# Sample attention: bias added on VectorE, fewer PE visits; prompt attention: v products of two steps together, in one PSUM bank

## The chip, the cores and the metric

The kernel runs on one core of a Trainium2 chip. The metric is the device time of one execution in microseconds. Three runs of the kernel before gave 2920.92, 2932.04 and 2932.24 us; their median, 2932.04 us, is the time before.

## What is computed

One layer of a hybrid decoder runs for two groups of tokens that share all weights: a prompt of 2048 tokens, and 8 samples of 8 new tokens each, which attend to 8192 cached tokens in a paged cache. Everything is float32; the projections are computed as three float32r products (high and low parts).

```python
h = rmsnorm(x, norm_g) * (1 + scale) + shift
z = h @ w_in                                  # one wide input projection, 8200 columns
pu, pg, q, k, v, fl, ag, ch, cb, cc, cg, mg = split_cols(z)
# forgetting attention, 8 heads of 64: for the prompt causal, for the samples over cache + new tokens
s = q @ k * scale + lq - lk                   # lk: cumulated log-forget values per cached row and head
p = softmax(where(k_pos <= q_pos, s, -inf)); o = p @ v
# pooling branch A, attention branch B, short convolution branch C
merged = sig(ga) * (ya @ w_br_a) + sig(gb) * (yb @ w_br_b) + sig(gc) * (yc @ w_br_c)
out = rmsnorm(x + gate * (merged @ w_o), final_g)
```

## The kernel before, in words

**First stage: projection and sample attention.** `project` streams the 2048 + 64 tokens through `w_in`, in two halves of the tokens: for each output tile of 128 columns and each of 8 input tiles three matmuls (L350 to L352, high by high, low by high, high by low). SP loads each weight tile (`raw`), ScalarE and VectorE split it. Behind this stream a generator, `decode`, computes the samples' attention over the cache. `pump` advances it in proportion to the projected columns; a scheduler with a simulated timeline then fixes each engine's order, by readiness and program order.

There are 64 decode steps, 8 per sample. A step takes 8 pages (1024 cached rows, 8 heads): two gathers of k (`kg`, issued by POOL), four VectorE transposes to `kt`, a bias (`nbt`), scores in PSUM bank dS, softmax, four TensorE transposes of the probabilities, `pT`, and then two halves (i = 0, 1) of products with four gathered v tiles each (`v`, POOL; `v_bufs` = 4 buffers) into bank dO. The bias of a row is written to DRAM as a high and a low part (`s_nbh`, `s_nbl`), loaded as 64 rows (`nbt`), and two matmuls with a selection matrix (L964) put it under the scores, which accumulate on it (L969). L964 is a 64 by 128 tile of the array; L969 and the v products (L995) are 128 by 32 tiles, four of which run side by side; the projection uses 128 by 128. The code has four yields per step: after the scores, after the softmax and the transposes, after each half of the products.

**Second stage: prompt attention with the A and C branches as filler.** `attention` runs 8 heads of 20 steps; TensorE's order here is written out by hand. A step handles two streams, each one 128-row tile of keys against a 512-column block Q of queries (stream 0: blocks 0 and 3, stream 1: blocks 1 and 2). At step i the code issues, in this order: the scores of step i + 1 (L1245, L1246, two PSUM banks `st`), three matmuls of the next head's maxima (L1170, three banks `mx`), twelve matmuls of a branch as filler (L1371 to L1373), and the v products of step i (L1263; stream 0 into bank oA, partitions 0 to 63, stream 1 into bank oB, partitions 64 to 127; each call is two machine matmuls). ScalarE exponentiates scores into `pt`; POOL and VectorE add `pt` into row sums `acc`. When a block is done, ScalarE copies it to `oT` (two buffers) and SP writes it to `s_o`. After the first step of the next head, `sums` reduces the `acc` tiles with ones (L1278) into an `mx` bank, ScalarE copies that to `ls`, which uses the same two buffers as `oT` (L1281). A head's q and k operands are four loads of 64 by 2048 (`head_loads`, L1150), into one of two whole sets.

**Third stage.** Branch B and the output projection; the change touches only where its first chunk starts.

The PSUM banks in the second stage are st 2, ac 1, oA 1, oB 1, mx 3: all eight.

Of the kernel before, what the change touches and what calls it, by code (L numbers as in the profile page):

```python
# [18 lines left out]
P = 128  # L19
# [20 lines left out]
class Mixer:  # L40
# [5 lines left out]
    def pools(self):  # L46
# [15 lines left out]
        self.s_nbh = dt("s_nbh", [NB * NPG, NH, P])  # L62
        self.s_nbl = dt("s_nbl", [NB * NPG, NH, P])
# [3 lines left out]
    def setup(self):  # L67
# [12 lines left out]
        self.ks = self.dp.tile([P, 4, NS], F32, name="ks")  # L80
        self.vs = self.dp.tile([NS, BW], F32, name="vs")
# [772 lines left out]
    def decode_consts(self):  # L854
        nc, dp = self.nc, self.dp

        sel = self.stage("sel")[0:64, 0:256].rearrange("p (a b) -> p a b", b=P)
        self.sel = dp.tile([64, 2, P], F32R, name="sel")
        for part in range(2):
            q = slice(32 * part, 32 * part + 32)  # L860
            nc.gpsimd.iota(sel[q], pattern=[[4, 2], [1, 4], [8, 4], [0, 8]], base=0, channel_multiplier=-1,
                           allow_small_or_imprecise_dtypes=True)
        nc.vector.tensor_scalar(out=self.sel, in0=sel, scalar1=0.0, scalar2=None, op0=ALU.is_equal)

# [3 lines left out]
        for g in range(4):  # L868
# [12 lines left out]
        nc.gpsimd.affine_select(out=self.tri, in_=self.tri, pattern=[[-1, P]], compare_op=ALU.is_gt, fill=0.0,  # L881
                                base=0, channel_multiplier=1)
        nc.vector.memset(self.tri[64:128, 0:64], 0.0)

    def decode_bias(self):
# [3 lines left out]
        nc.sync.dma_start(idxl, I["page_table"].rearrange("(n b) g -> (b g) n", n=4).bitcast(U32))  # L889
# [3 lines left out]
        for n in range(4):  # L893
# [18 lines left out]
            hi, lo = self.stage(f"nbh{n}", F32R)[:, 0:1024], self.stage(f"nbl{n}", F32R)[:, 0:1024]  # L912
            nc.scalar.copy(hi, nb)
            V.tensor_tensor(out=lo, in0=nb, in1=hi.bitcast(F32), op=ALU.subtract)
            for d, x in ((self.s_nbh, hi), (self.s_nbl, lo)):
                nc.sync.dma_start(d[n * P : (n + 1) * P].rearrange("n h t -> n (h t)"), x.bitcast(F32))

    def decode(self):

# [5 lines left out]
        NC = 8  # L925

# [9 lines left out]
        vs = values(0)  # L936
        qbd = dp.tile([P, 16, 32], F32, name="qbd")
        nc.gpsimd.memset(qbd, 0.0)
        for b in range(NB):
# [6 lines left out]
            stat = dp.tile([P, 2, 2, NC], F32, tag="stat", bufs=2, name=f"stat{b}")  # L946
            ob = dp.tile([P, 2, HD, NC], F32, tag="ob", bufs=1, name=f"ob{b}")
            for c in range(NC):
                nbt = dp.tile([64, 2, P], F32R, tag="nbt", bufs=2, name=f"nbt{b}_{c}")
                for part, d in ((0, self.s_nbh), (1, self.s_nbl)):  # L950
                    src = d[b * NPG + 8 * c : b * NPG + 8 * c + 8].rearrange("(t g) h x -> (g h) t x", g=4)
                    nc.sync.dma_start(nbt[32 * part : 32 * part + 32].bitcast(F32), src)
                kt = dp.tile([P, 2, 2048], F32, tag="kt", bufs=1, name=f"kt{b}_{c}")
                for i in range(2):
                    kg = dp.tile([P, 2048], F32, tag="kg", bufs=2, name=f"kg{b}_{c}_{i}")
                    t = b * 16 + c * 2 + i
                    ind(kg, ck, self.idxk[:, t : t + 1])
                    for x in range(2):
                        V.transpose(out=kt[:, i, x * D : (x + 1) * D], in_=kg[:, x * D : (x + 1) * D])  # L959
                ktv = kt.rearrange("p i (j x r) -> p i j x r", j=4, r=32)  # L960
                S = self.psum("dS")
                Sv = S.rearrange("p (a i x) -> p a i x", a=2, x=P)
                for hh in range(2):
                    nc.tensor.matmul(Sv[:, hh], self.sel[:, hh], nbt, start=(hh == 0), stop=False)  # L964
                for hh in range(2):
                    for dh in range(2):
                        for h4 in range(4):
                            x = (4 * hh + h4) * 2 + dh
                            nc.tensor.matmul(Sv[32 * h4 : 32 * h4 + 32, hh], qbd[:, x], ktv[:, :, :, x],  # L969
                                             start=False, stop=(hh == 1 and dh == 1))  # L970
                yield
                S3 = S.rearrange("p (a x) -> p a x", a=2)
                m, l = stat[:, 0, :, c], stat[:, 1, :, c]
                V.tensor_reduce(out=m, in_=S3, axis=AX.X, op=ALU.max)
                nm = dp.tile([P, 2], F32, tag="nm", bufs=2, name=f"nm{b}_{c}")
                V.tensor_scalar(out=nm, in0=m, scalar1=-1.0, scalar2=None, op0=ALU.mult)
                pr = dp.tile([P, 2, 256], F32, tag="pr", bufs=1, name=f"pr{b}_{c}")
                for hh in range(2):
                    nc.scalar.activation(out=pr[:, hh], in_=S3[:, hh], func=AF.Exp, bias=nm[:, hh : hh + 1],
                                         accum_out=l[:, hh : hh + 1])  # L980
                pt = self.psum("dT")
                for hh in range(2):
                    for i in range(2):
                        x = hh * 2 + i
                        nc.tensor.transpose(out=pt[:, x * P : (x + 1) * P], in_=pr[:, hh, i * P : (i + 1) * P],
                                            identity=self.ident)
                pT = dp.tile([P, 4, 4, 32], F32, tag="pT", bufs=1, name=f"pT{b}_{c}")
                nc.scalar.copy(pT.rearrange("p x g (h q) -> p x h g q", q=NQ),
                               pt.rearrange("p (x h g q) -> p x h g q", x=4, h=4, g=4))
                yield  # L990
                O = self.psum("dO")
                for i in range(2):

                    def product(hh, g):
                        return nc.tensor.matmul(O[32 * g : 32 * g + 32, hh * 256 : hh * 256 + 256],  # L995
                                                pT[:, 2 * hh + i, g], vs[g][:, hh * 256 : hh * 256 + 256],
                                                start=(i == 0 and hh == 0), stop=(i == 1 and hh == 1))


                    with self.tc.issue_after(product(0, 3).ins):  # L1000
                        for x in (0, 1, 2, 4, 5, 6, 7):
                            product(x // 4, x % 4)
                    if (b * NC + c) * 2 + i + 1 < NB * NC * 2:
                        vs = values((b * NC + c) * 2 + i + 1)
                    if i == 0:
                        yield
# [217 lines left out]
    def attention(self, filler):  # L1224
# [68 lines left out]
        for x, (h, i) in enumerate(steps):  # L1293
            if h + 1 < NH:
# [4 lines left out]
                if i == 4:  # L1299
                    self.head_loads(h + 1)  # L1300
# [283 lines left out]
```

## Time and profile before

| | us |
|---|---|
| median of three runs | 2932.04 |
| profiled execution, its own time | 2928.24 |
| its span (first to last instruction) | 2926.5 |
| first stage, 0 to 1966 | 1966.0, TensorE busy 1926.2 |
| second stage, 1966 to 2617.6 | 651.6, TensorE busy 604.2 |
| third stage, 2617.6 to the end | 308.9, TensorE busy 287.6 |

TensorE's mean granted clock is 0.981 of 2.4 GHz. "Busy" counts a matmul from its start to its modelled end, and matmuls overlap, so the cost of one is read from the distance to the next start: 0.23 us for 512 columns at the full clock, though the row says 0.39 us. A gap between starts that is longer than that is either a wait (in brackets at the row's end) or a cost of TensorE itself. The column PEclk of a stretch is the granted clock as a share of full speed.

### The profile page before, as it was taken

The page shows a single profiled execution, that of the slowest core. Times are in us where ns is not written, and L with a number is a line of the kernel's source. Part 1 is how long each engine was busy: PE and PEld are TensorE (multiplying, and loading weights), DVE is VectorE, ACT ScalarE, POOL GpSimd, SP SyncE. Part 2 cuts the span into 40 slices and gives each one's busy share as a digit, 9 for nine tenths or more (in the row PEclk, how much of TensorE's full clock was granted, in tenths as well). Part 3 has the DMA queues.
Part 4 walks back from the last instruction along what each step waited for, and adds up shares of the span by engine and source line. Part 5 has one row for each costly group of instructions (what it writes and reads, how often), then busy time and mean ns, then how long its engine had stood idle before and what let it go on. Part 6 is the DMA issues. An engine that isn't in the chain of part 4 may idle for free.

```text
span 2926.5 us, 45656 instructions
## 1 busy us (share of the span) xinstructions
PE 2818.0 (96%) x17611; PEld 2162.3 (74%) x17611; DVE 1524.8 (52%) x2732; ACT 771.0 (26%) x1546; POOL 1060.9 (36%) x1210
## 2 busy tenths in 40 slices
PE   7999999999999999999999999999999999989998
PEld 4778888788878887777777777775666566758886
DVE  5465654564343345466655533226655556645554
ACT  4322221222222332222112122213333333332221
POOL 1112344453444332344444432003433343424332
PEclk9999999999999999999999999999999899989999
DMA  6776667778777867977776775624455545247542
GB/s 224 249 222 209 206 222 239 231 241 270 247 256 255 272 192 246 299 233 234 241 237 226 257 230 154 161 83 134 115 142 137 146 123 134 85 125 221 172 142 82
DMA packets 397309, 577.55 MB, mean 197 GB/s; under 512 B 45639, under 2 KB 303351, under 8 KB 377611
## 3 DMA queue, kind: packets, MB, share of 16 engines
q1 hardware_dynamic: 337123, 304.05, 36.0%
q0 software_dynamic: 59968, 270.57, 27.1%
q8 instruction: 139, 2.28, 0.3%
q14 instruction: 79, 0.65, 0.1%
HBM read 478.82 MB, written 95.60 MB: 196 GB/s over the span
## 4 chain that ended last, share of the span: by engine, by line
PE 79%; DMA 11%; DVE 3%; issue 3%; POOL 2%; ACT 1%; SPq 1%; DVEq 0%; POOLq 0%; ACTq 0%
PE ps_a L350 15%; PE ps_a L351 15%; PE ps_a L352 15%; PE ps_dO L995 4%; PE ps_dS L969 4%; PE ps_oA L1263 4%; DMA v<-in_cache_v,idxv 3%; PE ps_st L1245 3%; PE ps_mx L1170 2%; PE ps_ac L1373 2%; PE ps_ac L1372 2%; PE ps_ac L1371 2%; PE ps_st L1246 2%; DMA s_o<-oT 2%; PE ps_u L1475 1%
## 5 line engine op out<-in xcount | busy, mean ns | idle before, releaser
L350 PE MATMUL ps_a<-h,whi 128*128 128x512 f32 (+2 forms) x2560 | 921.6, 360 | 3.2 <-ACT whi L326 1.5
L351 PE MATMUL ps_a<-h,wlo 128*128 128x512 f32 (+2 forms) x2560 | 911.4, 356 | 0.9 <-DVE wlo L327 0.9
L352 PE MATMUL ps_a<-h,whi 128*128 128x512 f32 (+2 forms) x2560 | 909.7, 356 | 0.2 <-POOL h L306 0.2
L923 POOL DMA_INDIRECT v<-in_cache_v,idxv x512 | 513.9, 1004 | 735.3 <-PE ps_dO L995 593.4
L350 PEld LDWEIGHTS ps_a<-h,whi 128*128 128x128 f32 x2560 | 483.2, 189 | 99.3 <-issue 34.2
L351 PEld LDWEIGHTS ps_a<-h,wlo 128*128 128x128 f32 x2560 | 483.6, 189 | 70.0 <-issue 11.5
L352 PEld LDWEIGHTS ps_a<-h,whi 128*128 128x128 f32 x2560 | 482.9, 189 | 70.9 <-issue 10.9
L327 DVE TENSOR_TENSOR wlo<-raw,whi 128x1024 fp32r<-128x1024 f32 x128 | 160.4, 1253 | 273.7 <-ACT whi L326 273.2
L959 DVE STREAM_TRANSPOSE kt<-kg 128x1024 f32<-128x1024 f32 x256 | 296.3, 1211 | 8.3 <-DMA kg<-in_cache_k,idxk 8.1
L1173 DVE TENSOR_REDUCE mx<-ps_mx 128x1 f32<-128x512 f32 (+3 forms) x288 | 159.0, 594 | 135.4 <-PE ps_mx L1170 134.4
L1268 POOL TENSOR_TENSOR acc<-acc,pt 128x512 f32<-128x512 f32 (+2 forms) x134 | 157.9, 1178 | 148.4 <-ACT pt L1251 128.5
L1251 ACT ACTIVATE pt<-ps_st 128x512 f32<-128x512 f32 (+3 forms) x288 | 141.0, 525 | 251.8 <-PE ps_st L1246 246.1
L923 POOL DMA_INDIRECT kg<-in_cache_k,idxk x128 | 130.2, 1017 | 200.8 <-DVE kt L959 112.7
L326 ACT CAST whi<-raw 128x1024 fp32r<-128x1024 f32 x128 | 133.8, 1046 | 163.6 <-PE ps_a L352 95.2
L669 ACT ACTIVATE mg<-ps_a 128x512 f32<-128x512 f32 (+2 forms) x120 | 62.7, 522 | 401.6 <-PE ps_a L352 394.1
L1245 PEld LDWEIGHTS ps_st<-qq,kk 128*128 128x128 f32 x320 | 61.7, 193 | 134.4 <-issue 109.6
L1371 PE MATMUL ps_ac<-gh,wh 128*128 128x264 f32 x512 | 150.6, 294 | 8.8 <-ACT wh L1326 5.3
L995 PE MATMUL ps_dO<-v,pT 128*32 128x256 f32 x2048 | 146.0, 385 | 9.8 <-DMA v<-in_cache_v,idxv 9.6
L1268 DVE TENSOR_TENSOR acc<-acc,pt 128x512 f32<-128x512 f32 (+2 forms) x154 | 104.8, 683 | 90.8 <-PE ps_oB L1263 48.8
L1373 PE MATMUL ps_ac<-gl,wh 128*128 128x264 f32 x512 | 149.5, 292 | 0.5 <-DVE gl L1327 0.5
L1372 PE MATMUL ps_ac<-gh,wl 128*128 128x264 f32 x512 | 149.5, 292 | 0.1
L969 PE MATMUL ps_dS<-kt,qbd 128*32 128x256 f32 x2048 | 147.8, 386 | 0.0
(357 smaller groups left out, 4137.8 us busy)
## 6 DMA issues: line engine op xcount, KB each, us to landing
raw<-in_w_in SPq DMA_DIRECT2D x128, 512.0 KB
s_mg<-mg SPq DMA_DIRECT2D x72, 256.0 KB
t<-s_mg SPq DMA_DIRECT2D x64, 264.0 KB
x<-in_x_prompt SPq DMA_DIRECT2D x32, 512.0 KB
s_m<-t SPq DMA_DIRECT2D x64, 132.0 KB
wc<-in_w_cond SPq DMA_DIRECT2D x16, 512.0 KB
v<-in_cache_v,idxv POOLq DMA_INDIRECT x512, 4.7
m<-s_m SPq DMA_DIRECT2D x64, 128.0 KB
```

What stands on the lines that cost most here:

```text
L327: nc.vector.tensor_tensor(out=lo, in0=raw, in1=hi.bitcast(F32), op=ALU.subtract)
L350: nc.tensor.matmul(acc, whi[:, k], hh, start=(k == 0), stop=False)
L351: nc.tensor.matmul(acc, wlo[:, k], hh, start=False, stop=False)
L352: nc.tensor.matmul(acc, whi[:, k], hl, start=False, stop=(k == KT - 1))
L923: ind = lambda out, src, idx: nc.gpsimd.indirect_dma_start(out=out, out_offset=None, in_=src, in_offset=bass.IndirectOffsetOnAxis(ap=idx, ...
L959: V.transpose(out=kt[:, i, x * D : (x + 1) * D], in_=kg[:, x * D : (x + 1) * D])
L969: nc.tensor.matmul(Sv[32 * h4 : 32 * h4 + 32, hh], qbd[:, x], ktv[:, :, :, x], start=False, stop=(hh == 1 and dh == 1))
L995: return nc.tensor.matmul(O[32 * g : 32 * g + 32, hh * 256 : hh * 256 + 256], pT[:, 2 * hh + i, g], vs[g][:, hh * 256 : hh * 256 + 256], s ...
L1268: e.tensor_tensor(out=acc[h, Q][:, lo:512], in0=acc[h, Q][:, lo:512], in1=pt[:, lo:512], op=ALU.add)
L1371: nc.tensor.matmul(y, wh[:, k, cols], hi[:, k], start=(k == 0), stop=False)
L1372: nc.tensor.matmul(y, wl[:, k, cols], hi[:, k], start=False, stop=False)
L1373: nc.tensor.matmul(y, wh[:, k, cols], lo[:, k], start=False, stop=(k == 3))
```

## The change

VectorE adds the bias: it is stored once, in float32 (`s_nb`), and loaded as a 128 by 512 tile by four DMAs, each of which reads 4 rows and repeats each 8 times (`nbt`, one buffer now). One `tensor_tensor_reduce` per half adds it to the scores in PSUM and takes the maximum; before, one `tensor_reduce` took the maximum of both. The selection matrix and its matmuls are gone. To make the score rows fit, the page order inside a step changes (`tri`, `idxl`, eight small loads).

A decode step has two yields: the first half of the previous step's products and this step's scores, then the second half of the products and this step's transposes. `issue_after` puts the later piece behind the earlier one on TensorE. `v_bufs` grows from 4 to 7. `ks`, `vs` and `n_o` lose their own buffers.

In the prompt's attention the v products of two steps are issued together, at odd i, into one bank `o` with the streams on its two partition halves; `sums` has a bank of its own (`l`) and comes at i = 1, before the products. q and k come in 512-column chunks from rings of five buffers; `pt` has 9 buffers instead of 5. In the A and C filler the B weights are loaded after the second set of A and C weights, not before, and branch B's first chunk waits six filler turns instead of four.

```diff
-            hi, lo = self.stage(f"nbh{n}", F32R)[:, 0:1024], self.stage(f"nbl{n}", F32R)[:, 0:1024]
-            nc.scalar.copy(hi, nb)
-            V.tensor_tensor(out=lo, in0=nb, in1=hi.bitcast(F32), op=ALU.subtract)
-            for d, x in ((self.s_nbh, hi), (self.s_nbl, lo)):
-                nc.sync.dma_start(d[n * P : (n + 1) * P].rearrange("n h t -> n (h t)"), x.bitcast(F32))
+            dst = self.s_nb[16 * n : 16 * n + 16].rearrange("c g h (a i x) -> i a (c g) h x", a=2, i=2)
+            for i in range(2):
+                for a in range(2):
+                    src = nb[64 * i : 64 * i + 64, 512 * a : 512 * a + 512]
+                    nc.sync.dma_start(dst[i, a], src.rearrange("p (h x) -> p h x", h=4))
...
+        def scores(k):
+            b, c = divmod(k, NC)
+            if c == 0:
+                queries(b)
+            nbt = dp.tile([P, 2, 256], F32, tag="nbt", bufs=1, name=f"nbt{k}")
+            for h4 in range(4):
+                nc.sync.dma_start(nbt[32 * h4 : 32 * h4 + 32].rearrange("p a x -> p (a x)"),
+                                  self.s_nb[k, :, h4].unsqueeze(1).broadcast_to([4, NQ, 4 * P]))
...
-                for hh in range(2):
-                    nc.tensor.matmul(Sv[:, hh], self.sel[:, hh], nbt, start=(hh == 0), stop=False)
...
-                V.tensor_reduce(out=m, in_=S3, axis=AX.X, op=ALU.max)
+            for hh in range(2):
+                V.tensor_tensor_reduce(out=S3[:, hh], in0=S3[:, hh], in1=nbt[:, hh], scale=1.0, scalar=-3 * BIG,
+                                       op0=ALU.add, op1=ALU.max, accum_out=m[:, hh : hh + 1])
...
+            with self.tc.issue_after(product(0, 3).ins):
+                for x in (0, 1, 2, 4, 5, 6, 7):
+                    last = product(x // 4, x % 4)
+            with self.tc.issue_after(last.ins):
+                then()
...
+        n = NB * NC
+        vs, pT = values(0), None
+        for k in range(n + 1):
+            run = lambda: None
+            if k < n:
+                S, nbt, run = scores(k)
+            if k:
+                O = self.psum("dO")
+                vs = products(k - 1, 0, pT, O, vs, run)
+            else:
+                run()
             yield
+            nxt = []
+            if k < n:
+                pr = softmax(k, S, nbt)
+                run = lambda: nxt.append(transposes(k, pr))
+            else:
+                run = lambda: nxt.append(None)
+            if k:
+                vs = products(k - 1, 1, pT, O, vs, run)
+                evict(k - 1, O)
+            else:
+                run()
+            pT = nxt[0]
+            yield
...
-    def head_loads(self, h):
-        nc = self.nc
-        r = slice(h * HD, (h + 1) * HD)
-        qq, kk = self.qq[h % 2], self.kk[h % 2]
-        for dst, src in ((qq[0:64], self.s_ql), (kk[0:64], self.s_kh), (qq[64:128], self.s_qh), (kk[64:128], self.s_kl)):
-            nc.sync.dma_start(dst.bitcast(F32), src[r])
+    def head_chunk(self, h, x, is_q):
+        r, c = slice(h * HD, (h + 1) * HD), slice(x * 512, x * 512 + 512)
+        ring, use, top, low = ((self.qq, self.qc, self.s_ql, self.s_qh) if is_q else
+                               (self.kk, self.kc, self.s_kh, self.s_kl))
+        t = use[h, x] = ring[len(use) % 5]
+        for dst, src in ((t[0:64], top), (t[64:128], low)):
+            self.nc.sync.dma_start(dst.bitcast(F32), src[r, c])
...
+        qload = {4: 0, 6: 1, 10: 3}
+        kload = {5: 0, 14: 1, 18: 2}
...
+                nc.tensor.matmul(O[64 * s : 64 * s + 64, lo:512], v[:, kt], pt[:, lo:512],
...
-            L = self.psum("mx")
+            L = self.psum("l")
...
+            if h and i == 1:
+                self.head_chunk(h, 2, True)
+                self.head_chunk(h, 3, False)
...
-            values(h, cur)
-            if i == 0 and h:
+            if i == 1 and h:
                 sums(h - 1, (0, 1, 2, 3))
-            if h == NH - 1 and i == 8:
+            if h == NH - 1 and i == 9:
                 sums(h, (0, 1))
                 self.early = True
+            if i % 2:
+                values(h, prev)
+                values(h, cur)
+            prev = cur
...
-    m.st_bufs, m.sc_bufs, m.v_bufs, m.pt_bufs, m.raw_bufs = 4, 8, 4, 5, 1
+    m.st_bufs, m.sc_bufs, m.v_bufs, m.pt_bufs, m.raw_bufs = 4, 8, 7, 9, 1
-    m.banks(two, "ps2", st=2, ac=1, oA=1, oB=1)
+    m.banks(two, "ps2", st=2, ac=1, o=1, l=1)
-            yield from m.branch_b(c, 0 if c else 4)
+            yield from m.branch_b(c, 0 if c else 6)
```

TensorE, first stage, decode step 11 (`kt` are its k tiles, `v` and `pT` those of the step before), before:

```order
L352 MATMUL ps_a<-h_665,whi_4645 128x256
L964 MATMUL ps_dS<-nbt_3_4877,sel 128x256 x2
L969 MATMUL ps_dS<-kt_3_4880,qbd 32x256 x13
L995 MATMUL ps_dO<-v_3_4627,pT_2_4745 32x256
L995 MATMUL ps_dO<-v_0_4621,pT_2_4745 32x256
L995 MATMUL ps_dO<-v_1_4623,pT_2_4745 32x256
L995 MATMUL ps_dO<-v_2_4625,pT_2_4745 32x256
L995 MATMUL ps_dO<-v_0_4621,pT_2_4745 32x256
L995 MATMUL ps_dO<-v_1_4623,pT_2_4745 32x256
L995 MATMUL ps_dO<-v_2_4625,pT_2_4745 32x256
L995 MATMUL ps_dO<-v_3_4627,pT_2_4745 32x256
L969 MATMUL ps_dS<-kt_3_4880,qbd 32x256 x3
```

and now:

```order
L353 MATMUL ps_a<-h_489,whi_4665 128x256
L1011 MATMUL ps_dO<-v_3_4725,pT_4717 32x256
L1011 MATMUL ps_dO<-v_0_4719,pT_4717 32x256
L1011 MATMUL ps_dO<-v_1_4721,pT_4717 32x256
L1011 MATMUL ps_dO<-v_2_4723,pT_4717 32x256
L1011 MATMUL ps_dO<-v_0_4719,pT_4717 32x256
L1011 MATMUL ps_dO<-v_1_4721,pT_4717 32x256
L1011 MATMUL ps_dO<-v_2_4723,pT_4717 32x256
L1011 MATMUL ps_dO<-v_3_4725,pT_4717 32x256
L977 MATMUL ps_dS<-kt_4824,qbd 32x256 x16
L354 MATMUL ps_a<-h_489,wlo_4666 128x256
```

The two L964 matmuls are gone, and the scores stand whole behind the first half of the products. In the whole program, visits of TensorE to the decode's scores and products (with L964, between rows of other work) go from 176 to 152.

TensorE, second stage, the start of head 1 (`acc` of head 0 are summed there), before:

```order
L1263 MATMUL ps_oA<-acc_0_18216,vh_16452 64x512
L1263 MATMUL ps_oB<-acc_1_18222,vh_16452 64x512
L1278 MATMUL ps_mx<-acc_0_17549,onesc 32x512
L1278 MATMUL ps_mx<-acc_1_17555,onesc 32x512
L1278 MATMUL ps_mx<-acc_2_17730,onesc 32x512
L1278 MATMUL ps_mx<-acc_3_17618,onesc 32x512
L1245 MATMUL ps_st<-qq_17544,kk_17545 128x256
L1246 MATMUL ps_st<-q_1_16431,k_1_16433 128x256
L1245 MATMUL ps_st<-qq_17544,kk_17545 128x512
L1246 MATMUL ps_st<-q_1_16431,k_1_16433 128x512
L1263 MATMUL ps_oA<-pt_0_1_18257,vh_16452 64x384
L1263 MATMUL ps_oB<-pt_1_1_18263,vh_16452 64x512
```

and now:

```order
L1303 MATMUL ps_st<-qq_17625,kk_17626 128x256
L1305 MATMUL ps_st<-q_1_16494,k_1_16496 128x256
L1303 MATMUL ps_st<-qq_16497,kk_17626 128x512
L1305 MATMUL ps_st<-q_1_16494,k_1_16496 128x512
L1335 MATMUL ps_l<-acc_0_17631,onesc 32x512
L1335 MATMUL ps_l<-acc_1_17637,onesc 32x512
L1335 MATMUL ps_l<-acc_2_17807,onesc 32x512
L1335 MATMUL ps_l<-acc_3_17694,onesc 32x512
L1320 MATMUL ps_o<-acc_0_18298,vh_16533 64x512
L1320 MATMUL ps_o<-acc_1_18304,vh_16533 64x512
L1320 MATMUL ps_o<-pt_0_1_18343,vh_16533 64x384
L1320 MATMUL ps_o<-pt_1_1_18349,vh_16533 64x512
```

The sums come after another group of scores, write bank l, and four v products follow them. Over the stage the visits to v products and sums go from 159 to 80; behind this place now stand four scores, three maxima and twelve filler matmuls before the next scores. At nine places two groups of scores stand without other matmuls between them (three groups at the start); before there was one.

SP's queue around the copies of finished blocks (`s_o`) at the end of head 0, before:

```order
L1150 DMA qq_17544<-s_ql 64x2048
L1139 DMA k_1_16433<-s_kh 64x2048
L1141 DMA k_1_16433<-s_nlkh 1x2048
L1141 DMA k_1_16433<-s_nlkl 1x2048
L1142 DMA q_1_16431<-s_qh 64x2048
L1378 DMA s_m<-t_1_18950 128x264
L1150 DMA kk_17545<-s_kh 64x2048
L1150 DMA qq_17544<-s_qh 64x2048
L1150 DMA kk_17545<-s_kl 64x2048
L1273 DMA s_o<-oT_3_19032 64x512
L1273 DMA s_o<-oT_2_19036 64x512
```

and now:

```order
L1202 DMA qq_16498<-s_ql 64x512
L1190 DMA k_1_16496<-s_kh 64x2048
L1192 DMA k_1_16496<-s_nlkh 1x2048
L1192 DMA k_1_16496<-s_nlkl 1x2048
L1193 DMA q_1_16494<-s_qh 64x2048
L1444 DMA s_m<-t_1_19038 128x264
L1202 DMA qq_16498<-s_qh 64x512
L1202 DMA kk_16502<-s_kh 64x512
L1202 DMA kk_16502<-s_kl 64x512
L1330 DMA s_o<-oT_3_19126 64x512
L1330 DMA s_o<-oT_2_19130 64x512
```

Four loads of 64 by 2048 for q and k (qq, kk) stood ahead of `s_o`; now two q loads and two k loads of 64 by 512 stand there. The loads of the maxima (k_1, q_1) stay.

## Rows read from the trace of the kernel before

**Rows 1.** Stretch us; busy PE, PEld, DVE, ACT, POOL; clock; DMA share; GB/s.

```profile
200.00:1800.00 1600.00, 1588.84 (x11122) 1244.87 (x11121) 818.71 (x1133) 374.57 (x806) 667.96 (x662) 1.00 0.73 238
...
1966.00:2617.60 651.60, 604.18 (x3216) 408.05 (x3216) 383.17 (x862) 227.05 (x415) 251.58 (x329) 0.94 0.47 125
```

**Rows 2.** TensorE's waits, 200 to 1800 us (total us, times, longest).

```profile
PE ps_dO L995 <- DMA v<-in_cache_v,idxv: 9.6, 13, 1.8
```

**Rows 3.** TensorE's waits in the second stage.

```profile
PE ps_mx L1170 <- ACT ls L1281: 20.8, 5, 5.8
...
PE ps_ac L1371 <- ACT wh L1326: 5.3, 1, 5.3
...
PE ps_st L1245 <- ACT acc L1251: 1.9, 2, 1.6
```

**Rows 4.** ScalarE at the start of head 1 (start, us, instruction, idle before).

```profile
2047.97 0.58 ACT L1272 COPY oT<-ps_oA 64x512 f32<-64x512 f32 x1 [1.21 <-PE ps_oB L1263]
...
2058.58 0.58 ACT L1281 COPY ls<-ps_mx 128x512 f32<-128x512 f32 x1 [4.56 <-DMA s_o<-oT]
```

**Rows 5.** Stretches of 16 us right behind waits of TensorE.

```profile
2059.00:2075.00 16.00, 15.78 (x74) 11.31 (x75) 9.08 (x26) 5.42 (x11) 3.86 (x6) 0.80 0.37 94
...
2315.00:2331.00 16.00, 15.86 (x64) 10.60 (x65) 6.81 (x19) 3.27 (x7) 4.95 (x7) 0.69 0.46 133
...
2474.00:2490.00 16.00, 15.44 (x82) 11.57 (x82) 11.18 (x29) 6.74 (x12) 4.75 (x7) 0.89 0.57 145
```

**Rows 6.** Timeline of TensorE, first stage: two visits of the decode.

```profile
600.53 0.31 PE L352 MATMUL ps_a<-h,whi 128*128 128x320 f32 x1
600.85 1.07 PE L995 MATMUL ps_dO<-v,pT 128*32 128x256 f32 x16
601.85 0.41 PE L350 MATMUL ps_a<-h,whi 128*128 128x320 f32 x1
602.10 0.30 PE L351 MATMUL ps_a<-h,wlo 128*128 128x320 f32 x1
...
603.12 0.31 PE L352 MATMUL ps_a<-h,whi 128*128 128x320 f32 x1
603.36 0.50 PE L964 MATMUL ps_dS<-nbt,sel 64*128 64x256 f32 x2
603.78 1.93 PE L969 MATMUL ps_dS<-kt,qbd 128*32 128x256 f32 x32
```

**Rows 7.** Timeline of TensorE, second stage: one visit to the v products.

```profile
2589.51 0.40 PE L1245 MATMUL ps_st<-qq,kk 128*128 128x512 f32 x1
2589.74 0.39 PE L1246 MATMUL ps_st<-q,k 68*128 68x512 f32 x1
2590.07 0.64 PE L1263 MATMUL ps_oA<-pt,vh 128*64 128x512 f32 x1
2590.07 0.64 PE L1263 MATMUL ps_oB<-pt,vh 128*64 128x512 f32 x1
2590.55 0.59 PE L1263 MATMUL ps_oA<-pt,vh 128*64 128x512 f32 x1
...
2591.07 0.50 PE L1245 MATMUL ps_st<-qq,kk 128*128 128x512 f32 x1
2591.41 0.40 PE L1246 MATMUL ps_st<-q,k 68*128 68x512 f32 x1
```

**Rows 8.** Groups of VectorE: busy us, mean ns, idle before.

```profile
L974 DVE TENSOR_REDUCE stat<-ps_dS 128x2 f32<-128x512 f32 x64 | 44.2, 690 | 91.8 <-PE ps_dS L969 91.4
...
L1175 DVE CUSTOM_DVE_ANT_0 ps_mx<-ps_mx,causal 128x128 f32<-128x128 f32 x128 | 36.8, 296 | 14.5 <-PE ps_mx L1170 13.6
```

**Rows 9.** Issue of a v gather, its landing (us), SP's queue (packets, MB, share).

```profile
L923 POOL DMA_INDIRECT v<-in_cache_v,idxv x512 | 513.9, 1004 | 735.3 <-PE ps_dO L995 593.4
...
q1 hardware_dynamic: 337123, 304.05, 36.0%
...
v<-in_cache_v,idxv POOLq DMA_INDIRECT x512, 4.7
```

More of the change, by code (lines that the diff above doesn't have):

```diff
@@ L934, in values, with queries @@
             return vs
[L936 to L939, printed above, removed]
+        def queries(b):
             qv = qbd.rearrange("p (f a) c -> p f a c", a=4)
@@ L977, in decode @@
[L977 to L991, printed above, removed]
-                for i in range(2):
[L994 to L1006, printed above, removed]
@@ L1007, in decode @@
-                om = dp.tile([P, 2, 4, HD], F32, tag="om", bufs=1, name=f"om{b}_{c}")
-                V.tensor_tensor(out=om, in0=O.rearrange("p (a h d) -> p a h d", a=2, h=4),
-                                in1=self.omask.unsqueeze(1).unsqueeze(3).broadcast_to([P, 2, 4, HD]), op=ALU.mult)
-                V.tensor_reduce(out=ob[:, :, :, c], in_=om.rearrange("p a h d -> p a d h"), axis=AX.X, op=ALU.add)
-                yield
+                                             start=(hh == 0 and dh == 0), stop=(hh == 1 and dh == 1))
@@ new lines, in scores, with softmax @@
+            return S, nbt, run
+        def softmax(k, S, nbt):
+            stat, c = seq[k // NC][0], k % NC
+            S3 = S.rearrange("p (a x) -> p a x", a=2)
+            m, l = stat[:, 0, :, c], stat[:, 1, :, c]
+            for hh in range(2):
+                V.tensor_tensor_reduce(out=S3[:, hh], in0=S3[:, hh], in1=nbt[:, hh], scale=1.0, scalar=-3 * BIG,
+                                       op0=ALU.add, op1=ALU.max, accum_out=m[:, hh : hh + 1])
+            nm = dp.tile([P, 2], F32, tag="nm", bufs=2, name=f"nm{k}")
+            V.tensor_scalar(out=nm, in0=m, scalar1=-1.0, scalar2=None, op0=ALU.mult)
+            pr = dp.tile([P, 2, 256], F32, tag="pr", bufs=1, name=f"pr{k}")
+            for hh in range(2):
+                nc.scalar.activation(out=pr[:, hh], in_=S3[:, hh], func=AF.Exp, bias=nm[:, hh : hh + 1],
+                                     accum_out=l[:, hh : hh + 1])
+            return pr
@@ new lines, in transposes @@
+        def transposes(k, pr):
+            pt = self.psum("dT")
+            for hh in range(2):
+                for i in range(2):
+                    x = hh * 2 + i
+                    nc.tensor.transpose(out=pt[:, x * P : (x + 1) * P], in_=pr[:, hh, i * P : (i + 1) * P],
+                                        identity=self.ident)
+            pT = dp.tile([P, 4, 4, 32], F32, tag="pT", bufs=1, name=f"pT{k}")
+            nc.scalar.copy(pT.rearrange("p x g (h q) -> p x h g q", q=NQ),
+                           pt.rearrange("p (x h g q) -> p x h g q", x=4, h=4, g=4))
+            return pT
@@ new lines, in products, with product @@
+        def products(k, i, pT, O, vs, then):
+            def product(hh, g):
+                return nc.tensor.matmul(O[32 * g : 32 * g + 32, hh * 256 : hh * 256 + 256],
+                                        pT[:, 2 * hh + i, g], vs[g][:, hh * 256 : hh * 256 + 256],
+                                        start=(i == 0 and hh == 0), stop=(i == 1 and hh == 1))
+            with self.tc.issue_after(product(0, 3).ins):
[3 more added lines that the diff above has]
+                then()
+            return values(2 * k + i + 1) if 2 * k + i + 1 < NB * NC * 2 else None
@@ L1082, in decode_finish @@
         sd = small[:, 0:64].rearrange("p (x d) -> p x d", d=4)
+        n_o = small[:, 512:1024]
+        nc.sync.dma_start(n_o, self.s_no)
         for b in range(NB):
@@ L1219, in start_attention @@
             self.head_max_loads(h)
-        self.head_loads(0)
+        for x in range(4):
+            self.head_chunk(0, (0, 1, 3, 2)[x], True)
+            self.head_chunk(0, x, False)
         self.head_values(0)
```

118 lines of the change are left out of this document (62 added, 56 removed).

## The prediction

> **What bounds the kernel now.** I read the stretches of the stages first, since one share of busy time would mix three stages. In the first stage TensorE is busy 1588.84 of 1600 us at the full clock, 2.4 GHz [rows 1]: this stage ends when TensorE's work ends, and only work taken off TensorE, or a cost between its matmuls, shortens it. The waits there are small: 9.6 us, in 13 pieces, for gathered v tiles [rows 2]. In the second stage TensorE is busy 604.18 of 651.60 us at a mean clock of 0.94 [rows 1], so both its waits and what they do to the clock count. The largest wait is 20.8 us for `ls`, the copy of the row sums, in five pieces; next comes 5.3 us for the split of new branch weights [rows 3]. Who ends the `ls` wait is read on ScalarE: at 2047.97 it copies a finished block to `oT`, and at 2058.58, after an idle 4.56 us, it copies `ls`; what ended the idle time is the DMA `s_o<-oT` [rows 4]. `ls` needs one of the two `oT` buffers, so it waits for the block's store; the maxima wait for the `mx` bank that `ls` has not yet emptied. After each such wait the clock is lower: 0.80 in the 16 us behind the first of the five, 0.89 behind the last, and 0.69 behind the wait for the weights [rows 5]. That means some time at 1.2 GHz in each.
>
> **The change part by part.** The sum is made on the profiled execution, 2928.24 us; the median of the runs shown is 3.80 us above it.
>
> *Selection products (first stage).* From 602.10 to 603.12 the starts of 320-column matmuls advance seven times, so one takes 0.146 us. The selection products start 0.24 us after the matmul before them, 0.09 more than that, and take 0.42 us to the start of the scores [rows 6]. Without them the array goes from the projection's tile to a 32-column tile directly, which shows at 600.85: 0.32 us after the start before it, 0.17 more than plain [rows 6]. Each step saves 0.09 + 0.42 - 0.17 = 0.34 us, 64 steps 22 us. Bounds: two plain matmuls of 256 columns (0.146 x 256/320 = 0.117 each) give 0.23 and 15 us; the whole 0.51 gives 33.
>
> *Fewer visits (first stage).* The order counts 176 visits before and 152 now. One costs 0.17 us on the way in and 0.25 - 0.146 = 0.10 on the way out [rows 6]; 24 of them 6.5 us. With the drain at the visit's end, which I do not see by itself, it may be 0.4 each, 10 us; below, 4.
>
> *Gathered v.* With 7 buffers three of the next half's four tiles can be loaded ahead. I take 3 of the 9.6 us [rows 2]; bounds: all 9.6, and the loss that the rival on `nbt` prices.
>
> *VectorE's addition.* It takes the place of a 690 ns reduction. A fused add and maximum over 128 columns takes 296 ns [rows 8]; over 256 columns it lies between that and 592, so two cost 0.6 to 1.2 us, at most 0.5 more per step. VectorE is busy 818.71 of 1600 us [rows 1], and projection matmuls stand between scores and transposes, so I cost it at nothing; without that cover it would be 64 x 0.5 = 32 us. The other edits of the first stage (split parts gone, eight small index loads, `n_o` through DRAM) lie under the same projection work.
>
> *v products of two steps (second stage).* Two plain 512-column starts lie 0.23 us apart (2589.51, 2589.74). The visit starts 0.33 after the last of them (0.10 too long), its two machine matmuls per stream take 0.48 and 0.52 (0.04 at the end), and the first score matmul afterwards takes 0.34 to the next start (0.11) [rows 7]: 0.25 us in all. The order has 159 visits before, 80 now: 79 x 0.25 = 20 us. Bounds: 0.20 and 0.30, 16 and 24. The two streams still start together, as oA and oB do at 2590.07 [rows 7].
>
> *Sums.* The wait of 20.8 us and the clock behind it: 0.20 x 16 = 3.2 us behind the first piece, 0.11 x 16 = 1.8 behind the last [rows 5], so about 2.5 each and 12.5 for five, 33 us in all. What is late next? `ls` still needs an `oT` buffer, and ScalarE still stops on it. But no `mx` bank hangs on it any more. TensorE meets it when it needs a score bank: in the new order that is behind four v products, four scores, three maxima and twelve filler matmuls. Before, it stopped 7.5 us after the `oT` copy; now it does one more group of scores (4 x 0.23) and one more maximum (0.23) first, and two to three groups of fillers, at 12 x 0.12 us each: 10 to 13 us after the copy. The store landed 10.6 us after it [rows 4]. And SP now has 1.6 MB of q and k loads queued before the store, where it had 3.1 (six loads of 64 x 2048 x 4 bytes; now two, and four of a quarter). I take 28 of the 33 us; bounds 17 and 33.
>
> *Weights of the filler's second half.* These are now loaded four filler turns ahead of their first product. The wait was 5.3 us [rows 3], the clock behind it 0.31 x 16 = 5.0 [rows 5]; I take 8 of the 10; bounds 0 and 10.
>
> *Adjacent scores.* At nine places two groups of scores now meet, and the second waits for ScalarE's exponentials. The rows have two such waits, 1.9 us together [rows 3]. In one of them ScalarE had other work, so I take 0.5 us each, 4 us lost; bounds 0 and 9.
>
> Third stage, branch B's start and the chunked loads: the chunks replace whole loads whose buffers came free at the head's end, and are asked for long before their use; I take 0.
>
> Sum: 22 + 6.5 + 3 + 20 + 28 + 8 - 4 = 83.5, and 2928.24 - 83.5 = 2844.7 us. I say 2844. With all terms at their good ends: 33 + 10 + 9.6 + 24 + 33 + 10 - 0 = 120, 2809 us; at their bad ends: 15 + 4 + 0 + 16 + 17 + 0 - 9 = 43, 2885 us, or 2890 with a little for VectorE's addition.
>
> **The rivals.** *The second stage's waits come back elsewhere.* ScalarE still stops at `ls`, and the two score banks hang on ScalarE; if the store is as late as before and the fillers are missing at that place, TensorE loses what it lost. Then 28 and 8 are not won: 2844 + 36 = 2880 us. For it: ScalarE's order is the same there. Against it: the 10 to 13 us above.
>
> *Slower: the bias load holds up the gathers.* One `nbt` load reads 4 rows and repeats each 8 times. If those four rows put it on four of the sixteen DMA engines, each takes 16 KB of its 64 KB. SP's queue moved 304.05 MB in 36.0% of 16 engines' span of 2926.5 us, which is 18.0 KB per us and engine [rows 9], so four loads keep those engines for 4 x 0.91 = 3.6 us per step. A v tile that is asked for behind them lands that much later. The slack of the second half's products: scores of 1.9 us [rows 6] and, late in the stage, 21 matmuls at 0.23 us, 6.7 us, against 1.0 us of issue and 4.7 us to landing [rows 9]: 1.0 us. So 2.6 us late in the worst case; at 2.3 on the mean 64 x 2.3 = 147 us, and 2844 + 3 + 147 = 2994. It decides from 87 / 64 = 1.4 us late per step. Against it: over the stage the four engines would go from a share of 0.73 [rows 1] by 64 x 3.6 / 1600 = 0.14 to 0.87, and the loads come once per step of some 25 us, mostly not beside the gather on which the products wait. The Trainium skill, "DMA: Bandwidth & Descriptors", section "Rules for kernel authors", states this rule: a leading broadcast dimension smaller than 16 confines a transfer to that many engines. No row here shows it, since no load of before has this shape; by it alone this rival would hold, and by the shares it would stay hidden.
>
> *Slower: one bank makes the two streams take turns.* Then the 0.48 and 0.52 of a visit's pair double. Full steps lose 1.0 us, steps on the diagonal less; over 160 steps some 136 us: 2844 + 136 = 2980. Against it: L995 writes four strips of one bank, and 16 of its matmuls start within 1.0 us (600.85 to 601.85 [rows 6]); in turns they could not.
>
> That the change does not do what it says is refuted by the order itself for the visits; for the waits it is the first rival.
>
> **How the numbers follow.** My forecast 0.82; the first rival 0.09; the bias load 0.05; one bank 0.04. The first two are faster by more than 0.5% (below 2917; half a per cent is about what a measurement of this kernel tells from no change). Of the bias load, 0.02 is a partial loss that ends within 0.5%, 0.03 slower; one bank is slower. So faster 0.91, same 0.02, slower 0.07. The range, 2812 to 2890, holds the forecast with its bounds and the first rival.
>
> **What would show it.** No L964 matmuls, and scores that start right behind the products without a gap; 80 visits to bank o, both streams starting together, two steps without a gap between; no wait for `ls`, and a mean clock near 0.97 or more in the second stage; the waits for v still under 15 us in all. I am wrong if TensorE waits for v or for `nbt`'s reader in most steps, if L1320's streams follow each other, or if new waits for scores add up to more than 20 us.

## The result, and the profile after

The changed kernel takes 2842.99 us (median of 4 runs, 2839.73 to 2845.51), the kernel before beside it 2928.64: a ratio of 0.971, 95% interval 0.9685 to 0.9735. The forecast was 2844, range 2812 to 2890. The profiled execution took 2839.73 us, 88.5 less than that of before; the sum of the prediction, made on that execution, gave 2844.7.

The stages after (per row: the stretch, its length, busy time of TensorE, weight loads, VectorE, ScalarE, GpSimd with instruction counts; granted clock, DMA share, GB/s):

```profile
0.00:1924.30 1924.30, 1886.16 (x12732) 1490.58 (x12733) 978.57 (x1683) 470.23 (x957) 698.89 (x775) 1.00 0.75 238
1924.30:2522.60 598.30, 574.40 (x3192) 402.88 (x3190) 386.48 (x857) 225.02 (x413) 262.98 (x328) 0.96 0.48 135
2522.60:2837.90 315.30, 289.17 (x1560) 246.56 (x1560) 165.46 (x379) 70.81 (x173) 110.08 (x108) 0.97 0.52 158
```

Cut at the same instructions, before had 1966.4, 652.3 and 307.8 us. So the first stage gave 42.1 (I had summed 31.5), the second 54.0 (52), and the third took 7.5 back (0). In the second stage TensorE's idle time fell by 23.5 us (47.4 to 23.9) and its busy time by 30.5 (604.9 to 574.4). Some 9 us of the latter are the clock, an estimate from the busy time at 1.2 GHz (57 us in the trace of before, 39 in this one).

TensorE's largest waits in the second stage after (who waits <- for whom: us, times, longest):

```profile
PE ps_st L1303 <- ACT pt L1310: 7.2, 10, 2.7
PE ps_mx L1222 <- DVE mx L1227: 3.9, 7, 0.9
PE ps_mx L1485 <- ACT gh L1392: 3.6, 1, 3.6
```

`ls` and `wh` of [rows 3] are gone; what is new, 7.2 us for the exponentials where adjacent scores meet, is 5.3 more than before. [rows 3] left out two waits of before, for the split of a branch's inputs (`gh`), the first of them at the start of branch B:

```profile
PE ps_mx L1419 <- ACT gh L1326: 7.6, 1, 7.6
PE ps_ac L1371 <- ACT gh L1326: 3.5, 1, 3.5
```

The first was the second largest wait of the stage. Together they fell from 11.1 to 3.6 us.

A first-stage visit after (start, duration, instruction), which answers to [rows 6]:

```profile
710.48 0.28 PE L355 MATMUL ps_a<-h,whi 128*128 128x256 f32 x1
710.60 0.28 PE L353 MATMUL ps_a<-h,whi 128*128 128x256 f32 x1
710.91 1.07 PE L1011 MATMUL ps_dO<-v,pT 128*32 128x256 f32 x16
711.76 1.94 PE L977 MATMUL ps_dS<-kt,qbd 128*32 128x256 f32 x32
713.63 0.39 PE L354 MATMUL ps_a<-h,wlo 128*128 128x256 f32 x1
```

The scores start 0.85 us after the products. In [rows 6] products alone took 1.00 until the next start, and scores behind selection products took a further 0.51 to begin.

A second-stage visit of two steps, answering to [rows 7]:

```profile
2050.59 1.94 PE L1320 MATMUL ps_o<-pt,vh 128*64 128x512 f32 x8
2052.46 0.50 PE L1303 MATMUL ps_st<-qq,kk 128*128 128x512 f32 x1
```

Eight matmuls of 512 columns take 1.87 us to the next start. One step's four took 1.00 in [rows 7], with the streams side by side, so two steps took 2.00; one after the other they would take 4.00. One bank does not make the streams take turns.

VectorE's new pair, which answers to [rows 8] (busy us, mean ns | idle before):

```profile
L986 DVE CUSTOM_DVE_ANT_0 ps_dS<-ps_dS,nbt 128x256 f32<-128x256 f32 x126 | 52.4, 416 | 136.2 <-DMA nbt<-s_nb 66.1 <-PE ps_dS L977 63.5 <-DMA s_ag<-g_ag 2.9
L986 DVE DVE_READ_ACCUMULATOR2_ANT stat<- 128x1 f32 x126 | 16.9, 134 | 0.2
```

Two of each take 1.10 us per step, 0.41 more than the 690 ns replaced. VectorE stops 66.1 us for `nbt` in this trace, hidden from TensorE, which waits 0.2 us for the probabilities (`pr`).

### The profile page after: what moved, and what is told of

Read it like the earlier page. It is cut to its first block, busy times and chain, and to the rows that moved or that the text cites. A ratio compares the mean times of both kernels' runs of the same rounds, so it can differ in the third digit from the quotient of the medians.

```text
span 2837.9 us, 45999 instructions
## 1 busy us (share of the span) xinstructions
PE 2749.7 (97%) x17483; PEld 2140.0 (75%) x17483; DVE 1530.5 (54%) x2919; ACT 766.1 (27%) x1543; POOL 1072.0 (38%) x1211
## 5 line engine op out<-in xcount | busy, mean ns | idle before, releaser
L1320 PE MATMUL ps_o<-pt,vh 128*64 128x512 f32 (+3 forms) x576 | 143.8, 553 | 0.0
L1303 PE MATMUL ps_st<-qq,kk 128*128 128x512 f32 (+2 forms) x320 | 128.8, 406 | 7.6 <-ACT pt L1310 7.2
L1325 DVE TENSOR_TENSOR acc<-acc,pt 128x512 f32<-128x512 f32 (+2 forms) x154 | 110.0, 719 | 43.2 <-POOL pt L1312 23.5
```

Source lines behind the costliest of these rows:

```text
L1325: e.tensor_tensor(out=acc[h, Q][:, lo:512], in0=acc[h, Q][:, lo:512], in1=pt[:, lo:512], op=ALU.add)
```

## The experiments

Runs 1 to 4 were made on one chip, 5 to 8 on a second, 9 to 12 on a third; which chip the first pair ran on is not recorded. Ratios are to the kernel before on the same chip, whose median was 2935.93 (runs 1 to 4), 2943.57 (5 to 8) and 2929.34 (9 to 12). Stage times compare within a chip.

**1. First stage alone.** Edit: the changed decode, with

```
-    m.st_bufs, m.sc_bufs, m.v_bufs, m.pt_bufs, m.raw_bufs = 4, 8, 7, 9, 1
+    m.st_bufs, m.sc_bufs, m.v_bufs, m.pt_bufs, m.raw_bufs = 4, 8, 7, 5, 1
```

and the attention, its loads and banks of before.

> The first stage's edits alone (bias added by VectorE, scores behind products, seven v buffers); the second stage as before. Theory A, the prediction's terms: 22 + 6.5 + 3 = 31.5 us less than before, about 2897 us. Theory B, read from the two traces since: the first stage ends 42 us earlier, all of it from these edits, because the selection products, full-array matmuls inside a visit, had made two more changes of tile shape per step that the count of 176 visits hides; then about 2887 us, and the second stage still 651 us long with its 21 us of waits for ls.

Measured 2918.28 us, ratio 0.9944 (0.9926 to 0.9963), 16 us less. Its first stage, and that of run 2, which has the old one on the same chip:

```profile
0.00:1955.60 1955.60, 1895.97 (x12732) 1494.53 (x12733) 972.67 (x1683) 470.06 (x957) 704.83 (x775) 0.99 0.73 234
```
```profile
0.00:1976.90 1976.90, 1929.91 (x12860) 1508.23 (x12861) 978.06 (x1496) 472.86 (x960) 703.94 (x774) 1.00 0.70 226
```

Busy time falls by 34 us, the stage by 21: idle time rises from 47.0 to 59.6. In the first pair busy time fell by 40 and idle time stayed (39.8, 38.1). Neither theory's number holds here; what TensorE no longer does is nearly the same in both, what it waits for is not. Gathered v is not the reason here: TensorE waits 22.8 us for it in run 2 and 16.4 in run 1. The added idle time is many small waits, the largest 3.5 us more for `pr`.

**2. Second stage alone.** Edit: the changed attention, loads and banks; decode of before, `v_bufs` 4.

> The second stage's edits alone (v products of two steps, one bank for both streams, sums in a bank of their own, loads in chunks); the first stage as before. If the parts are independent, the second stage shortens by 53 us and the third is 6 longer: 2929 - 47 = 2882 us, and this saving and that of the first stage alone add up to the 86 of the whole change. Prediction's terms: 20 + 28 + 8 - 4 = 52, 2877 us. Rival: part of the saving needs the first stage's new loads or pools, and the sum of the two falls short by more than 8 us.

2883.25 us, 0.9823 (0.9805 to 0.9842), 52 us less. With run 1 that is 68; run 4, which differs from the changed kernel in one bank only, shows 67 on this chip. The parts add up.

**3. A buffer for `ls`, in the kernel before.**

```
-            ls = ap.tile([P, 512], F32, tag="oT", bufs=2, name=f"ls{h}")
+            ls = ap.tile([P, 512], F32, tag="ls", bufs=1, name=f"ls{h}")
```

> The kernel before with one edit: the copy of the row sums, ls, has a buffer of its own and no longer needs one of the two oT buffers. Theory: the store of the finished block, for whose buffer ScalarE stops, is the cause of the 20.8 us wait and of the clock behind it, so 28 to 33 us go: 2896 to 2901 us, no wait for ls above 2 us, mean clock of the second stage 0.96 or more. Rival (the first one of the prediction): the wait comes back elsewhere, at the score banks or the exponentials, and the time stays above 2915 us.

2928.96 us, 0.9961 (0.9941 to 0.9981), 11 us less: the time is the rival's, not the theory's. The second stage is 636.5 us, 14.5 less than run 1's. TensorE's wait for `ls` is gone, but (TensorE's waits, then VectorE's):

```profile
PE ps_mx L1170 <- DVE mx L1173: 12.8, 5, 4.1
```
```profile
DVE rl L1285 <- DMA rl<-ls: 28.1, 6, 6.4
```

The store behind `ls` was the cause of that wait, and the next link in the same chain took its place: `rl`, read from `ls` by small DMAs. VectorE waited 7.4 us for them before and waits 28.1 now, and the maxima stand behind it. So the first rival was half right for this edit.

**4. Sums in the bank `mx` again.**

```
-            L = self.psum("l")
+            L = self.psum("mx")
```

> The changed kernel with one edit undone: the sums go into the mx bank of the maxima again instead of a bank of their own (the place in the order stays). Theory: the bank is what keeps ScalarE's stop at ls away from TensorE, so waits of the maxima for ls come back, 15 to 25 us with the clock behind them: 2858 to 2868 us. Rival: the later place (one step later, behind the fillers) and the fewer loads queued in front of the store are enough: within 4 us of 2843, and no wait for ls above 3 us.

2867.54 us, 0.9771 (0.9744 to 0.9798). The time is no verdict, since the first stage of this run is 29 us longer than in the first pair. The second stage is:

```profile
1953.30:2550.10 596.80, 570.22 (x3192) 400.51 (x3190) 385.84 (x857) 225.19 (x414) 262.79 (x328) 0.97 0.48 135
```

The stage takes 598.3 us without the edit (598.7 and 598.6 in runs 5 and 9), and there is no wait for `ls` above 0.3 us. The theory falls: the bank is not needed.

**5. The changed kernel again.** No edit.

> The changed kernel itself once more, beside the three others of this call, since the kernel before took 2929 us in the first runs and 2936 in the last. If what varies between the runs acts on both kernels alike, the ratio stays at 0.971, inside 0.9685 to 0.9735. Rival: the saving of the first stage depends on how late the gathered v tiles come (7 us of waits in the first trace, 16 to 19 in the later traces with the same first stage), and the ratio is above 0.974 where they come late.

2881.68 us, 0.9781 (0.9762 to 0.9801): the rival. First stage and its wait for v:

```profile
0.00:1971.90 1971.90, 1901.61 (x12732) 1496.51 (x12733) 975.93 (x1683) 469.47 (x957) 706.75 (x775) 0.99 0.73 232
```
```profile
PE ps_dO L1011 <- DMA v<-in_cache_v,idxv: 25.6, 17, 2.9
```

The same program idles 70.3 us here and 38.1 in the first trace, 18.6 of the difference at this one wait and 8.2 at `pr`; its second stage (598.7) is the same.

**6. Sums one step earlier.**

```
-            if i == 1 and h:
+            if i == 0 and h:
                 sums(h - 1, (0, 1, 2, 3))
```

> The changed kernel with one edit undone: the sums stand one step earlier, at the head's first step, as before; they keep their own bank. Freeing ls alone moved the stop from ScalarE to VectorE, whose reciprocal waited 30.2 us for rl, the small loads out of ls. Theory: the later place is what lets VectorE find rl loaded, so at the earlier place the wait for rl returns, 20 us or more, and TensorE waits 8 to 15 us for the maxima: 2852 to 2862 us where the changed kernel takes 2843. Rival: the chunked loads are what frees the queue; then within 4 us of the changed kernel and rl waits under 15 us.

2901.25 us, 0.9846 (0.9826 to 0.9866), 19 us over run 5; the second stage is 608.6, 9.9 longer. ScalarE's stop, here and in run 5:

```profile
ACT ls L1338 <- DMA s_o<-oT: 14.9, 4, 4.6
```
```profile
ACT ls L1338 <- DMA s_o<-oT: 5.4, 2, 3.0
```

The place matters, but not by the link I named: VectorE's wait for `rl` is 5.7 us, not 20. TensorE loses 3.4 more to the maxima and 1.4 to the exponentials. The order also has 87 visits in place of 80, since sums no longer stand next to products. That is worth about 1 us: with the stretches at 1.2 GHz counted half, busy time is 557 us in both traces. The 9.9 us are 2.9 of idle time and the rest nearly all the clock behind it (0.96; run 5: 0.97).

**7 and 11. The bias alone.** The old loops and four v buffers; the selection products out, VectorE adds. The cut shows the main lines; the new bias layout with its four loads per step and one buffer, the page order and the shared buffers of `ks`, `vs` and `n_o` belong to the edit too.

```
-                for hh in range(2):
-                    nc.tensor.matmul(Sv[:, hh], self.sel[:, hh], nbt, start=(hh == 0), stop=False)
...
-                V.tensor_reduce(out=m, in_=S3, axis=AX.X, op=ALU.max)
+                for hh in range(2):
+                    V.tensor_tensor_reduce(out=S3[:, hh], in0=S3[:, hh], in1=nbt[:, hh], scale=1.0, scalar=-3 * BIG,
+                                           op0=ALU.add, op1=ALU.max, accum_out=m[:, hh : hh + 1])
```

> The kernel before with the bias alone moved: VectorE adds it, no selection products; the loops, the visits and the four v buffers as before. Prediction's term: 64 x 0.34 = 22 us (15 to 33), so 0.9925 of before. If VectorE's two fused passes come onto the path, up to 32 us of that are lost and the ratio is 1.00 or more. If the bias load held up the gathers, the waits for v rise by more than 20 us above those of before on the same chip.

> The kernel before with the bias alone moved, as control for the next. It took 1.0076 of the kernel before with 51.1 us of waits for v; if the load of the bias is what costs, it does so on every chip: 1.000 to 1.012, with waits for v above 35 us.

2968.02 us, 1.0076 (1.0051 to 1.0101), and 2959.52, 1.0103 (1.0087 to 1.012): slower on both chips, with waits for v of 51.1 and 43.9 us. **12** is the same with the bias stored as sixteen rows and loaded at once:

```
-                for h4 in range(4):
-                    nc.sync.dma_start(nbt[32 * h4 : 32 * h4 + 32].rearrange("p a x -> p (a x)"),
-                                      self.s_nb[b * NC + c, :, h4].unsqueeze(1).broadcast_to([4, NQ, 4 * P]))
+                nc.sync.dma_start(nbt.rearrange("p a x -> p (a x)"),
+                                  self.s_nb[b * NC + c].rearrange("h g x -> (h g) x").unsqueeze(1).broadcast_to([16, NQ, 4 * P]))
```

> The kernel before with the bias alone moved, and the bias loaded by one load of sixteen rows. Theory: few rows and so few DMA engines were what held up the gathers; the waits for v fall from about 51 to 15 to 25 us, and the saving of the selection products shows: 0.988 to 0.996 of before, 30 us or more under its control. Rival: the four times larger bias (256 KB per step where it was 64 KB) or VectorE's second pass costs the time; then within 8 us of its control and waits for v above 40 us.

2938.73 us, 1.0039 (1.0021 to 1.0056), 21 under its control: less than the 30 expected, and no saving on before. The decode's set-up and its steps in run 11, then in run 12:

```profile
150.00:250.00 100.00, 99.69 (x686) 85.25 (x684) 54.50 (x111) 19.25 (x38) 16.04 (x23) 1.00 0.73 210
250.00:1700.00 1450.00, 1400.03 (x9881) 1095.53 (x9882) 764.79 (x1213) 341.31 (x737) 606.10 (x602) 0.99 0.77 245
```
```profile
150.00:250.00 100.00, 85.62 (x522) 74.26 (x520) 47.08 (x97) 16.58 (x33) 7.13 (x13) 0.91 0.58 167
250.00:1700.00 1450.00, 1426.30 (x10167) 1121.33 (x10167) 779.93 (x1237) 347.21 (x749) 623.20 (x619) 1.00 0.77 252
```

and their waits for v:

```profile
PE ps_dO L1000 <- DMA v<-in_cache_v,idxv: 43.9, 37, 3.0
```
```profile
PE ps_dO L1000 <- DMA v<-in_cache_v,idxv: 24.9, 26, 2.6
```

Same bytes per step, more rows: TensorE gains 26.3 us of busy time in the steps and waits 19.0 less for v. The set-up loses 14.1; my layout takes 64 stores in place of 16, which stand on SP's queue from 164 to 221 us. So four loads of four rows hold up the gathers more than one of sixteen; the number of loads changed with the rows, and the two were not tried apart. Whether 24.9 is still more than the old bias would cost here stays open: [rows 2] has 9.6, but runs 2 and 3, with the old bias and loops, wait 22.8 and 19.2 us on their chip.

**9 and 10. The changed kernel, and with the same sixteen-row load.**

> The changed kernel as control beside the next three. So far its first stage took 1924, 1953 and 1972 us in three traces with waits for v of 7, 19 and 26 us; if those waits and what hangs on them decide, this run lies between a ratio of 0.971 and 0.978 and its waits for v say where.

> The changed kernel with one edit: the bias of a step is stored so that its sixteen rows lie behind each other, and one load of 256 KB repeats each of sixteen rows eight times, in place of four loads that each repeat four rows. The bytes are the same. Theory: four rows put each load on few DMA engines, which hold up the gathers behind them (the prediction's rival on the bias load, in part); then the waits for v fall by 5 us or more and the time by 5 to 30 us beside the control. Rival: the bytes or the order of issue matter and not the rows; then within 4 us of the control.

2844.35 us, 0.9705 (0.9688 to 0.9721), with 5.8 us of waits for v, and 2858.41, 0.9752 (0.9735 to 0.9768). The control, then the edit:

```profile
150.00:250.00 100.00, 99.01 (x671) 85.09 (x670) 59.21 (x118) 19.46 (x42) 15.79 (x21) 1.00 0.75 221
250.00:1700.00 1450.00, 1438.47 (x10370) 1133.93 (x10369) 785.84 (x1251) 352.60 (x762) 654.39 (x650) 1.00 0.81 258
```
```profile
150.00:250.00 100.00, 81.04 (x497) 69.67 (x496) 46.55 (x97) 15.34 (x32) 8.11 (x13) 0.92 0.55 156
250.00:1700.00 1450.00, 1442.62 (x10448) 1138.87 (x10447) 795.91 (x1268) 351.66 (x761) 649.24 (x650) 1.00 0.80 260
```

The steps gain 4.2 us, the waits for v fall from 5.8 to 3.9 and VectorE's waits for `nbt` from 32.4 to none; the set-up loses 18. The time I expected was wrong because I had not priced those 48 more stores. Here new loops and seven buffers already hide all but a few us. Sixteen rows with a cheap set-up were not run, nor the edit on a chip with late gathers.

**8. v products in every step.**

```
-            if i % 2:
-                values(h, prev)
-                values(h, cur)
-            prev = cur
+            values(h, cur)
```

> The changed kernel with v products in every step again: 159 visits in the second stage in place of 80, one bank and all else as changed. Prediction's term: 79 x 0.25 = 20 us (16 to 24), so 2859 to 2867 us where the changed kernel takes 2843. Rival: visits are cheap, and the saving of the second stage is all in the waits and the clock: within 5 us of the changed kernel.

2898.94 us, 0.9843 (0.9826 to 0.9861), 17 over run 5. The second stage in one trace, and that of run 5:

```profile
1961.60:2566.10 604.50, 586.68 (x3192) 394.64 (x3190) 379.82 (x857) 226.97 (x414) 255.20 (x328) 0.98 0.47 133
1971.90:2570.60 598.70, 571.17 (x3192) 400.56 (x3190) 385.32 (x857) 225.17 (x413) 262.75 (x328) 0.97 0.48 135
```

Busy time is 15.5 us more, at a higher clock: busy time times clock is 575 us against 554, so some 20 us more work in 79 more visits, 0.26 each (an estimate from these two rows). Idle time is 9.7 less, so the stage shows 5.8 only. That execution took 2882.79, the fastest of five by 13 us; in all, undoing the pairs costs between 6 and 17 us.

## Why the prediction was right, and where it was not

The median came out 1 us from the forecast, the execution on which the sum was made 5 us from it, and in part by luck: the first stage gave 10.6 us more than was summed and the third lost 7.5. Below, work "at the full clock" is an estimate from the traces: starts of matmuls, waits left out, stretches at 1.2 GHz counted half.

- **Selection products (22).** About right. At the full clock TensorE's visits to scores and products take 322 us before and 297 with the bias alone (runs 7 and 11): 25 less (forecast 22). Busy time shows only 12.8 of it in run 11 (1913.8 against 1926.6), because TensorE spent 44 us of that stage at 1.2 GHz and 17 before. Run 12, whose order has 170 visits where run 11 has 173, has 290, so the line between this term and the next is not sharp.
- **Fewer visits (6.5).** This term was mis-sized most. At the full clock the visits take 281 us in the changed kernel and in run 9, 16 less than in runs 7 and 11 and 9 less than in run 12. The price, "0.17 us on the way in", was read from one visit (600.85 in [rows 6]). In 147 of the 176 visits before, the way in costs 0.11 us or less, as here:

```profile
634.46 0.31 PE L351 MATMUL ps_a<-h,wlo 128*128 128x320 f32 x1
634.70 1.07 PE L995 MATMUL ps_dO<-v,pT 128*32 128x256 f32 x16
```

That is 0.24 us between starts, 0.09 more than plain, and no more than the selection products' own way in [rows 6]; so they cost the whole 0.42 per step, 27 us. Left out was the 0.15 us that products save when scores follow at once (0.85 in place of 1.00). With 0.09, 0.10 and 0.15, 24 visits give 8 us, and the two terms 35 of the 41 us that the visits lost. The rest stays open: the groups of matmuls are also cut up differently inside the visits, which was not tried apart. Theory B of run 1 does not explain it: the selection products stand first in 65 of the 67 visits that hold them, and they are 64 by 128 tiles, not full-array ones.

- **VectorE's addition (0)** held in the first trace: 0.41 us more per step, under cover. In run 5 TensorE waits 8.4 us for `pr`; what makes it late there was not tested.
- **Gathered v (3) and the bias load.** 9.6 went to 7.0 and 5.8 us in two traces (25.6 in run 5). But the rival's mechanism was real in part. With the old loops and four buffers, run 11 is 30 us slower than the kernel before on its chip, although 25 us of work are gone. Its first stage is 1993.5 us, 27 longer than in the first trace of before: 40 us of new idle time and some 12 of clock, 0.8 per step where the rival had said 2.3. "Mostly not beside the gather" was wrong for four buffers; with the new loops the idle time is 37.7 (run 9). Which of loops and buffers does it was not tried apart. The Trainium skill, "DMA: Bandwidth & Descriptors", section "Rules for kernel authors", has the rule that a leading dimension under sixteen confines a transfer to at most that many engines; runs 11 and 12 agree in direction (43.9 to 24.9 us), though no row shows the engines themselves.
- **v products of two steps (20).** Right: some 20 at the full clock (run 8).
- **Sums (28), weights (8), adjacent scores (-4).** Together 32; idle time and clock gave 33. The parts differ. The wait for `ls` went entirely, but not by the step "no `mx` bank hangs on it any more": run 4 does without the bank. And "ScalarE still stops on it" hardly holds; its stop, before and after:

```profile
ACT ls L1281 <- DMA s_o<-oT: 29.0, 5, 8.1
```
```profile
ACT ls L1338 <- DMA s_o<-oT: 3.0, 1, 3.0
```

Run 6 shows the later place worth up to 10 us, with 14.9 us of that stop at the old place; run 3 shows that the chain of store, `ls` and `rl` stops TensorE at whichever link is left. The shorter loads on SP's queue, the third edit that acts on this chain, were not tried alone. The 5.3 us for `wh` are gone; the new wait for exponentials is 5.3 more than the old. The reading "next comes 5.3 us" overlooked the 7.6 us for `gh`: the waits for `gh` fell by 7.5 us, which no term had ("branch B's start" stood at 0), and new waits for VectorE took some 5 back. So this sum was right in part by luck. The clock of the second stage rose to 0.96 only, not 0.97.

- **Third stage (0).** Wrong by 7.5: 24 matmuls of branch B moved into it (1536 to 1560), and TensorE waits 14.0 us there for `tb`, with which VectorE empties branch B's bank; it waited 8.1 before. Not all of it belongs to the second stage's edits: runs 1 and 11, with the old order there, wait 13.2 and 12.8 us for `tb`, in third stages of 312.7 and 313.1 us. Why `tb` is later was not tested.

## What to carry to other kernels

Read the price of a visit from many visits, not from one, and look at what the groups inside it cost next to each other. Compare busy times only at the same clock; with the bias alone the idle time and a lower clock came together, and busy time showed half of the saving. Moving work off the bound engine can lose if its operands then come by larger loads; look at what shares the DMA engines with the gathers, and try one load of more rows before blaming its bytes. When a wait is removed, follow the same chain one link further before counting the wait as gone.

## What was not expected of the hardware

The same program, with nearly the same work, differs between sets of runs by what it waits for: 5.8 to 25.6 us for gathered v, 38 to 70 us of idle time in the first stage, 2843 to 2882 us in all. The traces of one set agree (65 to 76 us of idle time in runs 5, 6 and 8). Each set was made on one chip; whether the chip or something else of the set makes the difference was not separated. The kernel before varies less, 2929 to 2944, so the gain went from 86 us to 62.
